# A hybrid DeltaNet / gating / SwiGLU layer: the input projection wholly in two-part products

## The chip, the cores and the metric

One core of a Trainium2 chip runs the whole program in one launch. The time is that of the device in microseconds (us), the median of several executions. Engines are named as in the profile: PE (TensorE: matmul), PEld (its weight load), DVE (VectorE), ACT (ScalarE), POOL (GpSimd) and SP (SyncE), which here issues every DMA, in order.

## What is computed

One layer over 2304 tokens (256 of context, 2048 latent), width 1024. The part that the change touches is the first third: the modulation vectors, the modulated RMSNorm and the input projection.

```python
mod = (jax.nn.silu(c) @ w_ada + b_ada)[:, None, :]
sh1, sc1, g1, sh2, sc2, g2 = jnp.split(mod, N_MOD, axis=-1)
h = rmsnorm(x, norm1_g) * (1 + sc1) + sh1
proj = h @ w_in        # 1024 x 3088: q, k, v, z (512 each), u, vb (512 each), 16 gate logits
...                    # conv + gated DeltaNet scans, spatial gating
y = jnp.concatenate([y_a, y_b.astype(h.dtype)], axis=-1) @ w_out
x = x + g1 * y
h = rmsnorm(x, norm2_g) * (1 + sc2) + sh2
x = x + g2 * swiglu(h, w_gate, w_up, w_down)
```

## The kernel before, in words

**Tiles and passes.** Tokens are cut into 6 groups of 384 (three tiles of 128). `PASSES` walks through them in 8 passes of 24, 24, 24, 12, 12, 24, 12 and 12 *blocks*, 144 in all. A block (`block_mm`) is 128 output columns of `w_in` for one group: 8 steps of 128 over the contraction, summed in one PSUM bank `pd` of 384 to 388 columns. Six passes begin with the 16 gate logits (`plg`, function `logits`). In the first two passes 14 and 18 *modulation pieces* stand between the blocks: a piece is 128 rows of `w_ada` by 1024 columns, multiplied by the two conditioning vectors.

**Two kinds of product.** In steps 0 to 3 of a block the weights `wraw` and activations `hT0` are plain float32; the profile shows two matmul records for each such product. In steps 4 to 7 both are cut into two parts of type float32r (a high part by a cast, a low part by subtraction), and a product is three matmuls: high x high, low x high, high x low. The parts of the weights lie in `whl`, those of the activations in the two tiles `hT1`. In the trace all of these read `pd<-hT,wraw` (float32) and `pd<-hT,whl` (parts). The pieces of the first pass go in parts (`ada<-whl,wlg`), those of the second as float32 (`ada<-wraw,wl`).

**How weights come.** An item of the stream is a block or a piece. On its first use (36 blocks) 512 KB of `w_in` come into one of four `wraw` buffers, four items ahead (`s_load`), and `s_split` makes the parts of rows 512 to 1023: a cast on ACT or DVE, a subtraction on DVE or POOL, into one of four `whl` buffers. The parts are also written to DRAM (`wp`, 512 KB); k, q and v in pass 0, vb, u and z in pass 1. The other 108 blocks (*kept* below) read 256 KB of float32 rows and 512 KB of finished parts.

**Order.** All engines' instructions stand in an order that a planner makes while the program is built: `Model` holds a clock for each engine, steps of the side work (`spawn`) become due by it, and `tick` puts them between the matmuls of the blocks. That side work is the convolutions, the preparation of the DeltaNet chunks (`pk`, `px`), and the scans. `h_put` turns the next group's activations into matmul form: the first half while the last block of a pass is at step 4, the second half behind that block. After the passes come the output projection (from about 1250 us) and the FFN, from 1591 us to the end.

Of the kernel before, what the change touches and what calls it, by code (L numbers as in the profile page):

```python
# [9 lines left out]
F32 = mybir.dt.float32  # L10
# [6 lines left out]
KB = 8  # L17
# [10 lines left out]
NACC, NTH, NRB = 5, 4, 3  # L28
# [132 lines left out]
def hybrid_step(  # L161
# [367 lines left out]
    wlg = cA.tile([P, KB, P], F32R, name="wlg")  # L529

    wl32 = cA.tile([P, 4, P], F32, name="wl32")
    hal32 = cA.tile([P, 4, 20], F32, name="hal32")
    hal = [cA.tile([P, 4, 20], F32R, name=f"hal{i}") for i in range(2)]
    hT0 = cA.tile([P, 4, GT * P + 4], F32, name="hT0")
    hT1 = [cA.tile([P, 4, GT * P + 4], F32R, name=f"hT1{i}") for i in range(2)]

    with tc.manual_schedule():
# [95 lines left out]
        def ada_finish2(vec, mrow):  # L633
            if vec in (2, 5):
                vi = 0 if vec == 2 else 1
                for i in range(2):
                    pg = pt_("pg")
                    nc.tensor.matmul(pg[0:2], sel, mrow[:, i * 512:(i + 1) * 512], start=True, stop=True)
                    gs = A.tile([2, 512], F32, tag="tok", name="gs", bufs=3)
                    nc.scalar.copy(gs, pg[0:2])  # L640
                    nc.sync.dma_start(gv_d[vi, :, i * 512:(i + 1) * 512], gs)
# [48 lines left out]
        def h_put(g, hs, q):  # L690
            o = bo(g)
            ks = slice(4 * q, 4 * q + 4)
            for l in range(GT):
                c = slice(o + l * P, o + (l + 1) * P)
                if q:
                    nc.scalar.copy(hT1[0][:, :, c], hs[l][:, ks])
                    lighter(512, GP_BIAS_H).tensor_sub(hT1[1][:, :, c], hs[l][:, ks], hT1[0][:, :, c])
                else:
                    copy(hT0[:, :, c], hs[l][:, ks])
            for x, h in ((hT1[0], hal[0]), (hT1[1], hal[1])) if q else ((hT0, hal32),):  # L700
                if g:
                    nc.vector.tensor_copy(x[:, :, 0:2], h[:, :, (2 if g == 1 else 4 * (g - 1)):][:, :, 0:2])
                if 0 < g < NG - 1:
                    nc.vector.tensor_copy(x[:, :, o + GT * P:o + GT * P + 2], h[:, :, 4 * g + 2:4 * g + 4])
# [21 lines left out]
        DEPTH = 4  # L726
# [4 lines left out]
        wp_d = {first[kd] + P * i: dram.tile([P, 2, 512], F32, name=f"wp{kd}{i}") for kd in first for i in range(4)}  # L731

        halves = [(i, n) for i, it in enumerate(stream) for n in range(2)
                  if (not it[0] if it[1] == "ada" else n and it[0] <= kept_in(it))]
        place = {h: j for j, h in enumerate(halves)}

        def s_load(i):
            if i < len(stream):
                g, kind, a, c0 = stream[i]
                t = A.tile([P, KB, P], F32, tag="wraw", name="wraw", bufs=DEPTH)  # L740
                if kind != "ada" and g > kept_in(stream[i]):
                    assert not missing[wp_d[c0].name]
                    nc.sync.dma_start(t[:, 0:4], w_in[0:512, c0:c0 + P].rearrange("(k p) c -> p k c", p=P))
                    hl = A.tile([P, 2, 4, P], F32R, tag="whl", name="whl", bufs=4)
                    nc.sync.dma_start(hl[:].rearrange("p i k c -> p i (k c)").bitcast(F32), wp_d[c0])
                    raws[i], splits[i, 1] = t, (hl[:, 0], hl[:, 1])
                    return
# [7 lines left out]
        def s_split(j):  # L755

            if j < len(halves):
                i, n = halves[j]
                while i not in raws:
                    yield 200  # L760
                raw = raws[i]
                yield [raw]
                hl = A.tile([P, 2, 4, P], F32R, tag="whl", name="whl", bufs=4)
                hi, lo = hl[:, 0], hl[:, 1]
                copy(hi, raw[:, 4 * n:4 * n + 4])
                yield
                lighter(512, GP_BIAS if stream[i][0] else GP_BIAS_FIRST).tensor_sub(lo, raw[:, 4 * n:4 * n + 4], hi)
                splits[i, n] = (hi, lo)
                if stream[i][1] != "ada":
                    if stream[i][0] == kept_in(stream[i]):  # L770
                        store(wp_d[stream[i][3]], hl[:].rearrange("p i k c -> p i (k c)").bitcast(F32))
                elif n:
                    del raws[i]
                    yield
                    s_load(i + DEPTH)

        for i in range(DEPTH):
            s_load(i)
# [28 lines left out]
        def constants():  # L807
# [9 lines left out]
            nc.vector.tensor_copy(wlg, zr[:, None, :].to_broadcast([P, KB, P]))  # L817
            nc.vector.tensor_copy(wl32, zr[:, None, :].to_broadcast([P, 4, P]))
            nc.vector.tensor_copy(wl32[:, :, 0:2], cs[:, :, 0:4].rearrange("p c k -> p k c"))
            nc.vector.tensor_copy(wl32[:, :, 64:66], cs[:, :, 4:].rearrange("p c k -> p k c"))  # L820
            nc.vector.tensor_copy(wlg[:, :, 0:2], cs.rearrange("p c k -> p k c"))
            nc.vector.tensor_sub(wlg[:, :, 2:4], cs.rearrange("p c k -> p k c"), wlg[:, :, 0:2])
            yield [lraw]
            nc.vector.tensor_copy(wl32[:, :, 32:48], lraw[:, 0:4])
            nc.vector.tensor_copy(wlg[:, 4:, 32:48], lraw[:, 4:])
            nc.vector.tensor_sub(wlg[:, 4:, 48:64], lraw[:, 4:], wlg[:, 4:, 32:48])
# [15 lines left out]
        for j in range(3):  # L842
            spawn(s_split(j))
# [11 lines left out]
        def modulate(k):  # L855
            for c0, c1 in ((0, NP), (NP, NH + 20)):
                c = cx(c0 // P)
                n = min(c1, NH + 2)
                if k < 4:
                    act = k % 2 == 0  # L860
                    if act:
                        nc.scalar.activation(hT0[:, k, c0:n], xr[:, k, c0:n], AF.Identity,
                                             scale=mod[:, 0, c, k:k + 1], bias=mod[:, 1, c, k:k + 1])
                    else:
                        nc.vector.tensor_scalar(hT0[:, k, c0:n], xr[:, k, c0:n], mod[:, 0, c, k:k + 1],
                                                mod[:, 1, c, k:k + 1], op0=ALU.mult, op1=ALU.add)
                    continue
                nc.scalar.activation(hT1[0][:, k - 4, c0:n], xr[:, k, c0:n], AF.Identity,
# [5 lines left out]
        for k in range(KB):  # L874
            if k + 1 < KB:
                modulate(k + 1)
            if k >= 4:
                nc.vector.tensor_sub(hT1[1][:, k - 4, 0:NH + 2], xr[:, k, 0:NH + 2], hT1[0][:, k - 4, 0:NH + 2])
        for k in range(4):
            nc.scalar.activation(hal32[:, k], xr[:, k, NH:NH + 20], AF.Identity,  # L880
                                 scale=mod[:, 0, 0, k:k + 1], bias=mod[:, 1, 0, k:k + 1])
        nc.scalar.copy(hal[0], xr[:, 4:, NH:NH + 20])
        nc.gpsimd.tensor_sub(hal[1], xr[:, 4:, NH:NH + 20], hal[0])
# [1496 lines left out]
```

## Time and profile before

| | us |
|---|---|
| median of 3 runs (3088.43 to 3098.06) | 3096.82 |
| the profiled execution | 3100.84 |
| its span, first to last instruction | 3098.8 |
| of which the 144 blocks, from 48.2 to 1222.3 | 1174.1 |

Share of the span: PE 95% busy, PEld 82%, DVE 67%, ACT 43%, POOL 12%. A busy time counts an engine as busy from an instruction's start to its modelled end, so a PE that waits inside a run of overlapping matmuls may still count as busy. The DMA share is the busy time of the core's 16 DMA engines by that of 16 that never pause; in a full stretch it reads slightly over 1. PEclk is the granted TensorE clock, 1.00 being 2.4 GHz and 0.50 being 1.2 GHz.

### The profile page before, as it was taken

Reading aid. Unit: us, or ns where it says so; the run is one execution under the profiler, and the core shown is the slowest. Engines: PE = TensorE matmul, PEld = TensorE weight load, DVE = VectorE, ACT = ScalarE, POOL = GpSimd, SP = SyncE. Lnnn points to the kernel's source line nnn. Section 1 sums busy time; section 2 is a strip of 40 time slices with the busy share of each in tenths; the row PEclk is TensorE's granted clock in tenths of the full one; section 3 lists DMA queues with packets and bytes.
Section 4 is the critical chain, followed back from the end, with each engine's and each line's share of the span. In section 5 each row is a group of like instructions: output and inputs, shape, how many; then the busy total and the mean of one; then the engine's idle time right before and its main releaser. Section 6 shows DMA issues by size and latency. Waiting matters only on the chain. (4 is left out here: it accounts for less than half of the span.)

```text
span 3098.8 us, 45733 instructions
## 1 busy us (share of the span) xinstructions
PE 2941.6 (95%) x15379; PEld 2543.6 (82%) x15379; DVE 2077.9 (67%) x3882; ACT 1331.0 (43%) x3056; POOL 375.6 (12%) x551
## 2 busy tenths in 40 slices
PE   8989999999889999899969999999999999999998
PEld 3666777877667788798759999999999998888887
DVE  3767457476548675565588888777768866467666
ACT  4754445545646433243253333344333333344443
POOL 1121211211212111122222211000000000000000
PEclk9989999999989999899979999999999999999999
DMA  7978998887789988896537777877789956567764
GB/s 251 349 240 241 285 305 250 297 245 229 228 271 265 286 257 259 293 347 228 175 125 226 223 207 241 271 224 219 200 268 329 319 164 216 171 200 245 224 217 174
DMA packets 764442, 756.23 MB, mean 244 GB/s; under 512 B 93194, under 2 KB 610831, under 8 KB 762929
## 3 DMA queue, kind: packets, MB, share of 16 engines
q1 hardware_dynamic: 764209, 753.31, 77.9%
q8 instruction: 123, 2.02, 0.3%
q14 instruction: 110, 0.90, 0.1%
HBM read 539.27 MB, written 213.90 MB: 243 GB/s over the span
## 5 line engine op out<-in xcount | busy, mean ns | idle before, releaser
L149 PE MATMUL pm<-hb,wu 128*128 128x384 f32 x5544 | 992.3, 340 | 22.1 <-DMA hb<-hbd 8.0
L149 PEld LDWEIGHTS pm<-hb,wu 128*128 128x128 f32 x5544 | 978.7, 189 | 28.6 <-issue 8.9
L149 PE MATMUL pm<-un,ah 128*128 128x512 f32 x2079 | 478.7, 392 | 4.6 <-DVE ah L149 2.1
L149 PEld LDWEIGHTS pm<-un,ah 128*128 128x128 f32 x2079 | 391.9, 189 | 91.2 <-DVE ah L149 2.5
L149 PE MATMUL pd<-hT,wraw 128*128 128x384 f32 (+2 forms) x1152 | 435.5, 502 | 18.4 <-ACT rb L149 10.6
L149 DVE TENSOR_TENSOR wu<-ws,wu 128x512 fp32r<-128x512 f32 x448 | 321.2, 717 | 125.5 <-ACT wu L149 121.0
L149 PE MATMUL pd<-hT,whl 128*128 128x384 f32 (+2 forms) x1728 | 396.3, 371 | 6.7 <-DVE whl L149 6.7
L149 PEld LDWEIGHTS pd<-hT,whl 128*128 128x128 f32 x1728 | 311.6, 195 | 37.2 <-DVE whl L149 8.3
L149 PEld LDWEIGHTS pd<-hT,wraw 128*128 128x128 f32 x1152 | 208.5, 195 | 116.7 <-ACT rb L149 12.6
L149 ACT CAST wu<-ws 128x512 fp32r<-128x512 f32 x448 | 255.2, 616 | 20.5 <-DVE ws L149 20.5
L149 DVE TENSOR_TENSOR u<-u,pm 128x384 f32<-128x384 f32 x264 | 144.5, 547 | 19.9 <-PE pm L149 19.9
L149 ACT ACTIVATE s<-s 128x384 f32<-128x384 f32 x66 | 34.7, 525 | 258.1 <-DVE s L149 258.1
L149 DVE SCALAR_TENSOR_TENSOR acc<-rb,colT,acc 128x384 f32<-128x384 f32 (+1 forms) x252 | 138.9, 580 | 9.1 <-POOL acc L149 8.8
L149 DVE TENSOR_TENSOR ah<-ar,ah 128x1408 fp32r<-128x1408 f32 x63 | 102.3, 1623 | 55.9 <-ACT ah L149 54.7
L149 ACT ACTIVATE u<-u 128x384 f32<-128x384 f32 x66 | 34.7, 525 | 231.2 <-DVE u L149 231.2
L149 ACT CAST ah<-ar 128x1408 fp32r<-128x1408 f32 x63 | 86.4, 1372 | 108.3 <-PE pm L149 93.3
L149 DVE TENSOR_TENSOR un<-ur,un 128x512 fp32r<-128x512 f32 x154 | 99.5, 685 | 23.2 <-ACT un L149 23.2
L149 POOL TENSOR_TENSOR acc<-acc,th 128x384 f32<-128x384 f32 (+2 forms) x43 | 50.5, 1175 | 447.0 <-ACT th L149 436.1
L149 PE MATMUL po<-woa,yhi 128*128 128x512 f32 x288 | 101.8, 404 | 1.8 <-DVE tm L149 1.8
L149 PE MATMUL po<-wob,yhi 128*128 128x512 f32 x288 | 102.4, 408 | 0.0
L149 ACT CAST un<-ur 128x512 fp32r<-128x512 f32 x154 | 87.8, 615 | 19.4 <-DMA ur<-in_w_down_dram 8.7
L149 DVE TENSOR_TENSOR C<-C,pm 128x512 f32<-128x512 f32 x63 | 42.4, 685 | 79.1 <-PE pm L149 78.8
(303 smaller groups left out, 4148.4 us busy)
## 6 DMA issues: line engine op xcount, KB each, us to landing
ws<-ws SPq DMA_DIRECT2D x256, 256.0 KB
ar<-fa SPq DMA_DIRECT2D x63, 704.0 KB
ws<-in_w_gate_dram SPq DMA_DIRECT2D x128, 256.0 KB
wraw<-in_w_in_dram SPq DMA_DIRECT2D x108, 256.0 KB
ur<-wt SPq DMA_DIRECT2D x88, 256.0 KB
ws<-in_w_up_dram SPq DMA_DIRECT2D x84, 256.0 KB
fa<-u SPq DMA_DIRECT2D x99, 192.0 KB
x<-in_x_sample_dram SPq DMA_DIRECT2D x37, 512.0 KB
```

Source lines behind the costliest of these rows:

```text
L149: fn(*a, **k)
```

## The change

All 8 steps of a block use two-part products: 24 matmuls in place of 4 float32 products and 12 matmuls. `hT0` and the two `hT1` become four float32r tiles `hT[q][i]`, `hal32` goes, `modulate` and `h_put` make a high and a low part for both halves. Both halves of a weight block are split on its first use and both are stored (two stores of 512 KB); a kept block reads two times 512 KB of parts and no float32 rows. All modulation pieces multiply float32 (`wc32`, 4 columns of weights in place of 64), so those of the first pass are no longer split. The logits use parts only, with 32 columns in place of 128. `wraw` has two buffers in place of four, `whl` six (`NHL`) in place of four; a kept half is loaded as soon as six halves ago is used up (`s_next`), and a raw item when one of the two buffers comes free: a block's when both its halves are split, a piece's when PE has multiplied it.

```diff
-    wlg = cA.tile([P, KB, P], F32R, name="wlg")
...
-    hT0 = cA.tile([P, 4, GT * P + 4], F32, name="hT0")
-    hT1 = [cA.tile([P, 4, GT * P + 4], F32R, name=f"hT1{i}") for i in range(2)]
+    wlg = cA.tile([P, KB, 36], F32R, name="wlg")
+    wc32 = cA.tile([P, KB, 4], F32, name="wc32")
+    hal = [cA.tile([P, KB, 20], F32R, name=f"hal{i}") for i in range(2)]
+    hT = [[cA.tile([P, 4, GT * P + 4], F32R, name=f"hT{q}{i}") for i in range(2)] for q in range(2)]
...
-                if q:
-                    nc.scalar.copy(hT1[0][:, :, c], hs[l][:, ks])
-                    lighter(512, GP_BIAS_H).tensor_sub(hT1[1][:, :, c], hs[l][:, ks], hT1[0][:, :, c])
-                else:
-                    copy(hT0[:, :, c], hs[l][:, ks])
+                nc.scalar.copy(hT[q][0][:, :, c], hs[l][:, ks])
+                lighter(512, GP_BIAS_H).tensor_sub(hT[q][1][:, :, c], hs[l][:, ks], hT[q][0][:, :, c])
...
-        DEPTH = 4
-        wp_d = {first[kd] + P * i: dram.tile([P, 2, 512], F32, name=f"wp{kd}{i}") for kd in first for i in range(4)}
+        kept = lambda it: it[1] != "ada" and it[0] > kept_in(it)
+        plain = lambda it: it[1] == "ada"
+        wp_d = {first[kd] + P * i: dram.tile([P, 2, 1024], F32, name=f"wp{kd}{i}") for kd in first for i in range(4)}
...
+        def s_next(free=True):
+
+            taken[2] -= free
+            while taken[1] < len(halves) and taken[2] < NHL:
+                i, n = halves[taken[1]]
+                taken[1] += 1
+                taken[2] += 1
+                hl = A.tile([P, 2, 4, P], F32R, tag="whl", name="whl", bufs=NHL)
+                if kept(stream[i]):
+                    src = wp_d[stream[i][3]]
+                    assert not missing[src.name]
+                    nc.sync.dma_start(hl[:].rearrange("p i k c -> p i (k c)").bitcast(F32), src[:, n])
+                    splits[i, n] = (hl[:, 0], hl[:, 1])
+                else:
+                    spawn(s_split(i, n, hl))
+
+        for i in range(2):
+            s_load()
...
-                if k < 4:
-                    while i not in raws:
-                        idle()
-                    until(raws[i], hT0)
-                    nc.tensor.matmul(ps[:, :n], raws[i][:, k], hT0[:, k, c0:c0 + n], start=(k == 0), stop=False)
...
+                q, kk = divmod(k, 4)
+                while (i, q) not in splits:
+                    idle()
+                hi, lo = splits[i, q]
+                until(hi, lo, *hT[q])
+                for j, (w, x) in enumerate(((hi, hT[q][0]), (lo, hT[q][0]), (hi, hT[q][1]))):
+                    nc.tensor.matmul(ps[:, :n], w[:, kk], x[:, kk, c0:c0 + n], start=(k == 0 and j == 0),
+                                     stop=(k == KB - 1 and j == 2))
+                if kk == 3:
+                    del splits[i, q]
+                    s_next()
...
-                        if pi:
+                        if True:
...
-                            nc.tensor.matmul(ada_ps[n][0:64], wl32[:, k % 4, k // 4 * 64:k // 4 * 64 + 64],
+                            nc.tensor.matmul(ada_ps[n][0:4], wc32[:, k],
                                              raws[i][:, 4 * n:4 * n + 4].rearrange("p k c -> p (k c)"),
```

On PE in pass 0, around the first modulation piece that stands between two blocks, before (`hT_262` is the float32 tile, `hT_263` and `hT_264` are the high and the low part):

```order
L149 MATMUL pd<-hT_264,whl 128x386
L149 MATMUL ada_753<-whl,wlg 64x512 x2
L149 MATMUL ada_754<-whl,wlg 64x512 x2
L149 MATMUL pd<-hT_262,wraw 128x386 x4
L149 MATMUL pd<-hT_263,whl 128x386 x2
L149 MATMUL pd<-hT_264,whl 128x386
```

and now (`hT_261` and `hT_262` are the parts of the first half, `hT_263` and `hT_264` those of the second):

```order
L149 MATMUL pd<-hT_264,whl 128x386
L149 MATMUL ada_784<-wraw,wc_258 4x512
L149 MATMUL ada_785<-wraw,wc_258 4x512
L149 MATMUL pd<-hT_261,whl 128x386 x2
L149 MATMUL pd<-hT_262,whl 128x386
```

The piece is two float32 products in place of four on parts, and the block behind it begins with parts.

On SP at the start of the stream, before:

```order
L149 DMA lraw<-in_w_in_dram 128x8x16
L149 DMA wraw<-in_w_in_dram 128x8x128 x2
L149 DMA wraw<-in_w_ada_dram 128x1024
L149 DMA wraw<-in_w_in_dram 128x8x128
L149 DMA wpk_361<-whl 128x1024
L149 DMA wpk_362<-whl 128x1024
```

and now:

```order
L149 DMA lraw<-in_w_in_dram 128x8x16
L149 DMA wraw<-in_w_in_dram 128x8x128 x2
L149 DMA wpk_361<-whl 128x1024 x2
L149 DMA wpk_362<-whl 128x1024 x2
L149 DMA wraw<-in_w_ada_dram 128x1024
L149 DMA wraw<-in_w_in_dram 128x8x128
```

The third and the fourth item stood ahead of the first stores, and now stand behind four of them.

On SP in pass 1, where kept blocks and pieces alternate, before:

```order
L149 DMA wraw<-in_w_in_dram 128x4x128
L149 DMA whl<-wpq_367 128x1024
L149 DMA wraw<-in_w_ada_dram 128x1024
L149 DMA wraw<-in_w_in_dram 128x4x128
L149 DMA whl<-wpq_368 128x1024
```

and now:

```order
L149 DMA whl<-wpq_365 128x1024 x2
L149 DMA wraw<-in_w_ada_dram 128x1024
L149 DMA whl<-wpq_366 128x1024 x2
L149 DMA wraw<-in_w_ada_dram 128x1024
L149 DMA mrow<-in_b_ada_dram 1x1024
```

The 256 KB of float32 rows have gone, and the parts are read two times 512 KB a block.

## Rows read from the trace of the kernel before

**Rows 1.** The page, part 1: busy time, share of the span, instructions.

```profile
PE 2941.6 (95%) x15379; PEld 2543.6 (82%) x15379; DVE 2077.9 (67%) x3882; ACT 1331.0 (43%) x3056; POOL 375.6 (12%) x551
```

**Rows 2.** Windows by pass: stretch, length, busy of each engine, PEclk, DMA share, GB/s.

```profile
48.20:238.10 189.90, 168.60 (x708) 124.28 (x707) 127.46 (x296) 122.37 (x320) 34.20 (x62) 0.92 0.85 277
238.10:446.50 208.40, 204.92 (x952) 144.45 (x952) 115.25 (x235) 98.33 (x238) 40.51 (x77) 0.98 0.93 282
446.50:634.80 188.30, 178.88 (x997) 147.96 (x996) 115.30 (x248) 90.47 (x253) 35.77 (x66) 0.98 0.86 266
634.80:719.50 84.70, 81.58 (x431) 64.81 (x429) 70.78 (x154) 44.87 (x123) 9.93 (x7) 1.00 0.81 231
719.50:829.70 110.20, 95.99 (x478) 77.58 (x479) 56.99 (x137) 60.29 (x182) 19.59 (x48) 0.92 0.78 245
829.70:1009.90 180.20, 162.12 (x808) 129.16 (x806) 116.30 (x251) 101.49 (x262) 36.52 (x51) 0.95 0.86 259
1009.90:1104.10 94.20, 89.72 (x494) 74.74 (x495) 65.81 (x120) 42.71 (x91) 15.62 (x37) 0.96 0.90 270
1104.10:1222.30 118.20, 117.78 (x788) 104.27 (x788) 70.24 (x142) 32.92 (x73) 22.85 (x71) 1.00 0.84 262
```

**Rows 3.** What PE waited for from 48 to 1222 us: total, times, longest (us).

```profile
PE px L149 <- DMA wbd<-w: 14.9, 6, 6.8
...
PE pd L149 <- DVE whl L149: 6.7, 3, 5.7
```

**Rows 4.** The same for SP's DMA queue.

```profile
SPq L149 <- PE pd L149: 242.2, 125, 8.9
```

**Rows 5.** PE in order of time, pass 1: start, length, what, count.

```profile
277.05 1.31 PE L149 MATMUL pd<-hT,whl 128*128 128x386 f32 x6
278.19 2.75 PE L149 MATMUL pd<-hT,wraw 128*128 128x386 f32 x8
280.49 2.56 PE L149 MATMUL pd<-hT,whl 128*128 128x386 f32 x12
282.98 1.93 PE L149 MATMUL ada<-wraw,wl 128*64 128x512 f32 x4
284.85 0.55 PE L149 MATMUL ptr<-ident,acc 128*128 128x128 f32 x3
```

**Rows 6.** PE in order of time, pass 0: a modulation piece in parts.

```profile
83.21 1.09 PE L149 MATMUL ada<-whl,wlg 128*64 128x512 f32 x4
84.14 2.76 PE L149 MATMUL pd<-hT,wraw 128*128 128x386 f32 x8
```

**Rows 7.** The chain of waits, in the FFN: start, length, what.

```profile
2290.99 298.83 PE pm L149 x1692
```

**Rows 8.** DMA issues of the run: what, count, KB each.

```profile
wraw<-in_w_in_dram SPq DMA_DIRECT2D x108, 256.0 KB
...
whl<-wpk SPq DMA_DIRECT2D x20, 512.0 KB
...
wpk<-whl SPq DMA_DIRECT2D x4, 512.0 KB
```

**Rows 9.** Windows with the DMA engines full, columns as in rows 2.

```profile
100.00:150.00 50.00, 48.77 (x223) 36.25 (x222) 33.05 (x81) 38.46 (x114) 5.23 (x13) 1.00 1.05 352
1300.00:1400.00 100.00, 99.04 (x701) 91.30 (x701) 59.59 (x155) 41.71 (x168) 26.72 (x21) 1.00 1.03 344
```

**Rows 10.** Tile `whl`, 48 to 1222 us: ns min/median/max; last, idle before splits.

```profile
L149 DVE TENSOR_TENSOR whl<-wraw,whl x52: 675/684/1115, 55.2 to 432.7; 128x512 fp32r<-128x512 f32 x52
L149 ACT CAST whl<-wraw x33: 602/615/636, 54.5 to 407.8; 128x512 fp32r<-128x512 f32 x33
...
  DMA wraw<-in_w_in_dram: 7.5, 5
```

**Rows 11.** ACT in order of time where pass 0 begins.

```profile
46.39 5.38 ACT L149 ACTIVATE hT<-xr,mod 128x256 f32<-128x256 f32 x12 [1.65 <-DVE mod L149]
```

**Rows 12.** PE in order of time where pass 6 begins.

```profile
1009.92 2.20 PE L149 MATMUL pd<-hT,wraw 128*128 128x384 f32 x6 [1.26 <-ACT hT L149]
```

More of the change, by code (lines that the diff above doesn't have):

```diff
@@ L725, in hybrid_step, with s_load @@
         raws, splits = {}, {}
-        DEPTH = 4
         second = next(pi for pi in range(1, len(PASSES)) if PASSES[pi][1] != "delta")
         kept_in = lambda it: second if it[1] in ("vb", "u", "z") else 0
-        wp_d = {first[kd] + P * i: dram.tile([P, 2, 512], F32, name=f"wp{kd}{i}") for kd in first for i in range(4)}
[L733 to L738, printed above, removed]
-                g, kind, a, c0 = stream[i]
[L740 to L747, printed above, removed]
+        kept = lambda it: it[1] != "ada" and it[0] > kept_in(it)
+        plain = lambda it: it[1] == "ada"
+        wp_d = {first[kd] + P * i: dram.tile([P, 2, 1024], F32, name=f"wp{kd}{i}") for kd in first for i in range(4)}
+        whole = [i for i, it in enumerate(stream) if not kept(it)]
+        halves = [(i, n) for i, it in enumerate(stream) if not plain(it) for n in range(2)]
+        taken = [0, 0, 0]
+        def s_load():
+            if taken[0] < len(whole):
+                i = whole[taken[0]]
+                taken[0] += 1
+                g, kind, a, c0 = stream[i]
+                t = A.tile([P, KB, P], F32, tag="wraw", name="wraw", bufs=2)
                 if kind == "ada":
@@ L753, in s_load @@
                 raws[i] = t
-        def s_split(j):
-            if j < len(halves):
-                i, n = halves[j]
-                while i not in raws:
[L760 to L765, printed above, removed]
-                yield
[L767 to L775, printed above, removed]
@@ L777, in hybrid_step, with s_split @@
-        for i in range(DEPTH):
-            s_load(i)
+        def s_split(i, n, hl):
+            while i not in raws:
+                yield 200
+            raw = raws[i]
+            yield [raw]
+            hi, lo = hl[:, 0], hl[:, 1]
+            copy(hi, raw[:, 4 * n:4 * n + 4])
+            yield
+            lighter(512, GP_BIAS if stream[i][0] else GP_BIAS_FIRST).tensor_sub(lo, raw[:, 4 * n:4 * n + 4], hi)
+            splits[i, n] = (hi, lo)
+            if stream[i][1] != "ada" and stream[i][0] == kept_in(stream[i]):
+                store(wp_d[stream[i][3]][:, n], hl[:].rearrange("p i k c -> p (i k c)").bitcast(F32))
+            if n:
+                del raws[i]
+                yield
+                s_load()
@@ L841, in hybrid_step @@
         spawn(constants(), set_up)
-        for j in range(3):
-            spawn(s_split(j))
+        s_next(False)
         for vec in (1, 0):
@@ L876, in hybrid_step @@
                 modulate(k + 1)
[L877 to L883, printed above, removed]
+            nc.vector.tensor_sub(hT[k // 4][1][:, k % 4, 0:NH + 2], xr[:, k, 0:NH + 2], hT[k // 4][0][:, k % 4, 0:NH + 2])
+        nc.scalar.copy(hal[0], xr[:, :, NH:NH + 20])
+        nc.gpsimd.tensor_sub(hal[1], xr[:, :, NH:NH + 20], hal[0])
         phP.close()
@@ L1481, in logits @@
                     def logits(k):
[L1482 to L1489 removed]
+                        q, kk = divmod(k, 4)
+                        until(*hT[q])
+                        for i in range(2):
+                            nc.tensor.matmul(pl[0:32, :nrow], wlg[:, k, 0:32], hT[q][i][:, kk, o:o + nrow],
+                                             start=(k + i == 0), stop=(k + i == KB))
                         if k % 2:
```

81 lines of the change are left out of this document (23 added, 58 removed).

## The prediction

> **What bounds the kernel now.** I read the page first: PE is busy 95% of the span [rows 1], and no other engine comes near. The change lies in the blocks of passes 0 to 7, so the windows by pass come next [rows 2]. The reader is to see two things in them. PE is the busiest engine in every pass, at 87 to 100% of its length; DVE has a sixth to a half of its time free and ACT a third or more. And the DMA share, 0.78 to 0.93, leaves little: where the engines are full, the share reads 1.03 to 1.05 at 344 to 352 GB/s [rows 9], so 335 GB/s is one full share. Length times share gives the DMA time of passes 0 to 7: 161, 194, 162, 69, 86, 155, 85 and 99 us, 1011 in all. PE's own waits are short: 15 us for `wbd`, which the preparation reads back, 7 us for `whl` [rows 3]. SP in turn waited 242 us for PE to free a buffer [rows 4]: loads are issued as soon as there is room, and their landing is hidden by how far ahead they go. So PE sets the pace, with the DMA engines close behind.
>
> **The change part by part: PE.** In a clean block the float32 half starts at 278.19, the half in parts at 280.49, the next thing at 282.98: 4.79 us for 386 columns [rows 5]. The new block is 24 products in parts. One end of their price is the FFN's undisturbed run, 298.83 us by 1692, 0.177 us each [rows 7], 4.24 us a block. The other is a short run of this projection, six products behind a transpose, 278.19 - 277.05 = 1.14 us, 0.19 each [rows 5], 4.56 us. The saving is 0.23 to 0.55 us a block; I take 0.48 (0.18 a product), since 24 products in a row are nearer to the long run. 144 blocks: -69 us, with bounds of -33 and -79. The logits of a pass trade 4 float32 products (2.3 us to the next start, 2.75 to their own end [rows 5], so some 2.5) for 8 in parts (1.4), -1.1 each, six times, -7. A modulation piece in parts takes 84.14 - 83.21 = 0.93 us [rows 6], as float32 284.85 - 282.98 = 1.87 [rows 5]: 14 pieces, +13. Sum on PE: -63; by pass 0, -13, -13, -7, -7, -13, -6, -6 (the logits counted where they stand, the 13 us of the pieces in pass 0).
>
> **DMA.** The 108 kept blocks drop a read of 256 KB and add one of 512 KB (`whl` is read 108 times now, in six groups like the one shown) [rows 8]: +256 KB each, 0.78 us at 335 GB/s. The 24 stores of parts double (six groups of four): +512 KB, 1.57 us each. Lower prices are possible, since the dropped rows were short pieces; higher ones too, since pass 1 moves only 282/0.93 = 303 GB/s per share. Added time by pass: 12 stores 19; 12 kept and 12 stores 28; 24 kept 19; 12 kept 9; 9; 19; 9; 9: 122 us. The DMA time becomes 180, 222, 181, 78, 95, 174, 94, 108.
>
> **The sum.** PE alone would need 190, 196, 176, 78, 103, 168, 88 and 112 us. At a share of 1.05 the transfers need 171, 211, 172, 74, 90, 166, 90, 103; the later of the two in each pass adds up to 1128, against 1174 now: -46. At a share of 1.00 the sum is 1154, -20. A whole pass has never run at 1.05, and one reached 0.93, so both ends are hopeful; I take the middle, -33.
>
> **DVE, ACT and SP.** Pass 0 splits 24 more halves of blocks and 28 fewer of pieces, pass 1 12 more; at 0.62 for the cast and 0.68 for the subtraction [rows 10] that is 16 us of work in 208, on two engines half free: nothing, unless a split comes late (below). At each of the 7 changes of group three subtractions are added (0.68 each), and the four float32 steps (2.5 us) that cover the second half's casts become 2.1 us. The change to pass 6 already shows 1.26 us of waiting for `hT` [rows 12]. I put 0.7 us on each, +5; the bounds are 0 and 2.5 (all of it bare). At the start ACT makes 16 in place of 12 activations, 7.2 in place of 5.4 us [rows 11], and DVE 8 more operations, but the first block also gets shorter: nothing, within 2 us. SP loses one issue and gains one in a kept block. In passes 0 and 1 raw buffers fall from four to two, and a store can stand ahead of the next load: +6 here, bounds 0 and 50 (third rival).
>
> Sum: -33 + 5 + 6 = -22 us. From the profiled execution, 3100.84 (its span of 3098.8 and 2 us around it), that is 3079; the median of the runs shown is 4.0 below it, so 3075. The output projection and the FFN are left as they are.
>
> **Rivals.** *First, PE's whole saving arrives.* For it: in the window from 100 to 150 us the share is 1.05 and PE still works 48.77 of 50 us at full clock, and so from 1300 to 1400 [rows 9]; three blocks of parts stand ready, some 20 us of PE. It needs the added transfers to go into the quarter of the DMA time that is idle now. Price: -63 + 3 = -60, 3037. The Trainium skill, "DMA: Bandwidth & Descriptors", section Specifications, limits a core to about 358 GB/s of its memory, which the 352 in rows 9 agrees with. By that figure pass 1 would need (58.8 + 9.4) MB / 358 = 190 us, less than PE's 196, and the time would be this rival's.
>
> *Second, the DMA engines take it all.* The passes' shares stop at about 0.96, since SP issues in order and waits in front of buffers: 1133/0.96 = 1180 us against 1174, with the +5 and some of PE's cover, 3097 to 3108. That the change doesn't do what it says ends here too: in passes full of side work, products in parts at 0.19 us each save only 0.23 a block, -33 + 6, and the DMA costs eat the rest.
>
> *Third, the shorter look-ahead costs more than all that, slower.* Place: passes 0 and 1, behind modulation pieces. A piece keeps one of the two `wraw` buffers until PE has multiplied it; the next block's load is then issued, has to land, be cast (0.62) and subtracted (0.68), within the block and the piece that are left to PE, 4.3 + 1.9 = 6.2 us. Four buffers deep, splits already stood idle for `wraw` 7.5 us in five waits [rows 10], and PE 6.7 us for `whl` [rows 3]. A load of 512 KB takes 1.6 us at full share, behind whatever is queued. If load and split together take 6.2 us nothing is lost; at 7.3 us, 1.1 us on each of some 23 such places (14 pieces in pass 0, 9 in pass 1) makes 25 us and brings the time back to before, and from there on the kernel is slower. At 8.3 us it is 48 us, 3117. Against it: side work on PE lengthens a block to 7.9 us in pass 0 and 8.7 in pass 1 [rows 2].
>
> **How the numbers follow.** The forecast, part of the saving (3055 to 3088), has a chance of 0.37; the first rival (3030 to 3055) 0.17; the second (3088 to 3106) 0.19; the third (3106 to 3150) 0.27. A measurement of this kernel tells about 0.3%, 9.3 us, from no change, so below 3087.5 is faster, above 3106.1 slower: 0.53, 0.20, 0.27. The likeliest gives 3075. For 8 in 10 the range leaves out the lower third of the first rival and about half of the third: 3036 to 3124.
>
> **What would show it.** Blocks of 4.3 us with no float32 products; DMA shares of 0.95 to 1.02 in passes 1, 2, 5 and 6, with pass 1 no shorter than now and passes 2 to 7 some 5 us shorter each. The first rival shows in shares of 1.02 and more in all passes and a pass 1 of 196 us; the second in PE's waits for DMAs (`wbd`, `skq`) growing from 15 us to 50; the third in waits of `pd` for `whl` in passes 0 and 1, with both longer than before, and a lower PEclk there. I am wrong in the main if pass 1 falls clearly, or if passes 2 to 7 grow.

## The result, and the profile after

The changed kernel takes 3145.25 us (median of 4 runs, 3143.51 to 3146.22), the kernel before 3097.44 beside it: a ratio of 1.0158, with an interval from 1.0135 to 1.0181. It is slower by 48 us, where 22 us less were forecast. (Such intervals, at 95%, stand in square brackets below.) Its page, part 1 (busy time, share of the span, instructions), answers to [rows 1]:

```profile
PE 2910.0 (93%) x15955; PEld 2638.3 (84%) x15955; DVE 2103.9 (67%) x3915; ACT 1339.4 (43%) x3049; POOL 397.2 (13%) x566
```

PE is busy 32 us less, in a span 44 us longer. Where the time went shows in the windows by pass of the changed kernel, which answer to [rows 2] (stretch, length, busy of PE, PEld, DVE, ACT, POOL, PEclk, DMA share, GB/s); the last row is the stage from the last block to the FFN:

```profile
48.30:275.20 226.90, 179.03 (x803) 137.76 (x801) 138.94 (x311) 128.65 (x321) 42.46 (x72) 0.90 0.87 282
275.20:498.20 223.00, 199.80 (x1038) 158.23 (x1038) 123.98 (x248) 99.33 (x242) 43.22 (x80) 0.95 0.90 287
498.20:685.90 187.70, 175.44 (x1163) 170.52 (x1163) 106.21 (x246) 93.52 (x260) 32.08 (x64) 0.97 0.94 313
685.90:783.30 97.40, 76.98 (x439) 73.40 (x439) 74.15 (x154) 48.54 (x134) 18.32 (x21) 0.89 0.78 235
783.30:885.70 102.40, 92.18 (x586) 87.75 (x585) 64.22 (x157) 59.65 (x164) 23.53 (x44) 0.93 0.92 309
885.70:1059.40 173.70, 151.44 (x872) 145.60 (x870) 120.27 (x240) 98.68 (x254) 35.08 (x44) 0.92 0.96 300
1059.40:1147.40 88.00, 82.44 (x516) 79.77 (x515) 61.11 (x114) 39.15 (x83) 19.75 (x39) 0.96 0.94 292
1147.40:1262.90 115.50, 105.56 (x742) 104.39 (x743) 67.74 (x133) 30.77 (x66) 20.69 (x66) 0.96 0.83 261
1262.90:1639.70 376.80, 335.83 (x1958) 291.49 (x1956) 224.09 (x448) 131.66 (x420) 94.63 (x80) 0.94 0.75 250
```

Against [rows 2], pass 0 is 37 us longer, pass 1 15, pass 3 13. Passes 2 and 4 to 7 are 1, 8, 7, 6 and 3 us shorter. The stage behind the passes (368.5 us before) is 8 us longer, the FFN 5 shorter. The blocks themselves did become shorter; a run of PE without a break, in order of time (start, length, what):

```profile
1021.74 6.09 PE L149 MATMUL pd<-hT,whl 128*128 128x384 f32 x33
```

That is 0.185 us a product with the last one counted to its own end (a product by itself takes a median of 0.338 us), or 0.180 from one start to the next: 4.32 to 4.43 us for a block's 24 of 384 columns, where the clean block before, of 386, took 4.79 [rows 5]. PE's waits grew. In pass 0 PE now waits for the splits (total, times, longest, us), 6.7 us before [rows 3]:

```profile
PE pd L149 <- DVE whl L149: 25.6, 16, 4.9
```

And the tile `wraw` in pass 0 of the changed kernel tells why these are late (loads with their count; what the engines that use it sat idle for, us and times; then the time from issue to landing, least, median and longest):

```profile
L149 SPq DMA_DIRECT2D wraw<-in_w_in_dram x21: 368/384/1145, 58.0 to 255.5; - x21
L149 SPq DMA_DIRECT2D wraw<-in_w_ada_dram x15: 327/333/986, 67.4 to 269.1; - x15
...
  DMA wraw<-in_w_in_dram: 45.2, 21
...
DMA to landing us min/median/max: 4.0/5.4/8.7
```

36 loads in 226.9 us through two buffers: each buffer takes a new load every 12.6 us on average, and of these the load itself takes 5.4 by the median.

### The profile page after: what moved, and what is told of

Same layout as the page of the kernel before. It is cut to its first block, busy times and chain, and to the rows that moved or that the text cites. A ratio compares the mean times of both kernels' runs of the same rounds, so it can differ in the third digit from the quotient of the medians.

```text
span 3143.1 us, 46924 instructions
## 1 busy us (share of the span) xinstructions
PE 2910.0 (93%) x15955; PEld 2638.3 (84%) x15955; DVE 2103.9 (67%) x3915; ACT 1339.4 (43%) x3049; POOL 397.2 (13%) x566
## 5 line engine op out<-in xcount | busy, mean ns | idle before, releaser
L149 PE MATMUL pd<-hT,whl 128*128 128x384 f32 (+2 forms) x3456 | 729.3, 360 | 67.5 <-DVE whl L149 27.8
L149 PEld LDWEIGHTS pd<-hT,whl 128*128 128x128 f32 x3456 | 629.5, 198 | 98.0 <-DVE whl L149 27.6
L149 POOL TENSOR_TENSOR ws<-ws 128x512 f32<-128x512 f32 x40 | 63.2, 1580 | 263.3 <-DMA ws<-in_w_up_dram 155.4
L149 PE MATMUL ph<-ident,x 128*128 128x128 f32 x336 | 55.9, 294 | 32.8 <-DVE x L149 14.6
```

The costliest lines, as they stand in the source:

```text
L149: fn(*a, **k)
```

## Experiments on the buffers

Six kernels change only what lies between the loads and PE. Theory: passes 0 and 1 are longer since two raw buffers look less far ahead than four. Rivals: the splits are late by themselves, or the stores of parts fill the DMA engines.

**e1**, the changed kernel with four raw and four half buffers:

```diff
-NACC, NTH, NRB, NHL = 5, 4, 3, 6
+NACC, NTH, NRB, NHL = 5, 4, 3, 4
...
-                t = A.tile([P, KB, P], F32, tag="wraw", name="wraw", bufs=2)
+                t = A.tile([P, KB, P], F32, tag="wraw", name="wraw", bufs=4)
```

> The changed kernel with four raw buffers again and four halves of parts in place of two and six (the same memory). If the short look-ahead for raw weights behind modulation pieces made passes 0 and 1 longer (+37 and +15 us in the profiles), they return to some 190 and 200 us and the time is 3085 to 3105. If it is the added DMA traffic or the splits on DVE and ACT, passes 0 and 1 stay at 220 to 227 and 215 to 223 us, and the time stays within 10 us of 3145, or rises since kept blocks have only four halves ahead.

Measured: 3151.6 us, ratio 1.0195 [1.0178, 1.0212]. Its windows (columns as above; passes 0 and 1, pass 5, the stage behind the passes):

```profile
49.10:234.30 185.20, 164.55 (x804) 127.02 (x803) 120.63 (x278) 117.56 (x307) 43.97 (x68) 0.96 0.95 319
234.30:454.50 220.20, 196.74 (x997) 155.97 (x996) 122.07 (x243) 102.22 (x250) 47.05 (x83) 0.92 0.91 289
...
842.60:1052.50 209.90, 168.16 (x974) 161.24 (x972) 129.47 (x274) 102.90 (x260) 35.19 (x61) 0.90 0.89 271
1250.80:1638.00 387.20, 342.21 (x2022) 299.08 (x2021) 228.92 (x459) 133.96 (x425) 97.51 (x90) 0.93 0.75 248
```

Pass 0 comes back, 185.2 us, shorter than before. Pass 1, which was to come back too, stays at 220.2: more raw buffers do not mend it. And 36 us more in pass 5 and 10 behind the passes take it away again: the FFN starts at 1638.0, in the changed kernel at 1639.7. **e2** (the pieces of pass 0 in parts again), **e3** (two buffers for pieces, two for blocks) and **e4** (one of the two stores, the other half's parts used twice) are variants of the same question:

```diff
-        plain = lambda it: it[1] == "ada"
+        plain = lambda it: it[1] == "ada" and it[0]
...
-                t = A.tile([P, KB, P], F32, tag="wraw", name="wraw", bufs=2)
+                t = A.tile([P, KB, P], F32, tag=("wraw", "araw")[c], name="wraw", bufs=2)
...
-            if stream[i][1] != "ada" and stream[i][0] == kept_in(stream[i]):
+            if n and stream[i][1] != "ada" and stream[i][0] == kept_in(stream[i]):
```

> The changed kernel with the pieces of pass 0 in parts again, as before the change (buffers two and six). Look-ahead theory: a piece of pass 0 no longer keeps a raw buffer until PE comes to it, so pass 0 falls by 20 to 35 us, pass 1 does not change: 3110 to 3125. If the float32 pieces cost only their own time on PE, pass 0 falls by 13 us at most: 3132 or more. If the splits on DVE and ACT are what is late, pass 0 grows (28 more halves): above 3145.

> The changed kernel with two buffers for the pieces and two for raw blocks, each loaded in its own order, and four halves of parts: no piece can keep a block's buffer. Look-ahead theory: passes 0 and 1 as with four raw buffers or better, 3085 to 3100. If it is DMA traffic or splits: 3135 to 3155.

> The changed kernel, but only the second half of the parts is stored (24 stores of 512 KB as before the change), and kept blocks read that half twice; so their first four steps use the wrong weights. DMA theory: 19 us less transfer in each of passes 0 and 1, and the time falls by 20 to 38 us, to 3107 to 3125. Look-ahead theory: the stores are not what is waited for, the time falls by 0 to 8 us.

Measured: 3160.21, 3178.02 and 3163.31 us, 15, 33 and 18 more than the changed kernel; e3 and e4 lie above everything that was expected of them. With the pieces of pass 0 in parts (e2) that pass falls by 7 us only, to 220.1, and the rest of the kernel loses more. Pass 0 falls to 196.4 us with buffers of their own for the pieces (e3), and again nothing is left of it at the end. 12.6 MB of stores less gain nothing (e4): that rival falls.

**e5** joins both sizes of the look-ahead: four raw and four half buffers until the last raw item, then all eight for halves.

```diff
+                tag = "wraw" if taken[1] > last and (taken[1] - last) % 2 else "whl"
+                if flight[tag] + (len(raws) if tag == "wraw" else 0) >= 4:
+                    break
...
-                hl = A.tile([P, 2, 4, P], F32R, tag="whl", name="whl", bufs=NHL)
+                hl = A.tile([P, 2, 4, P], F32R, tag=tag, name="whl", bufs=4)
```

> Four buffers for raw items and four for halves as long as items come raw (passes 0 and 1), and from the last raw item on all eight hold halves (a half then goes by turns into a former raw buffer). Nothing is left out. Look-ahead theory: both sizes of the look-ahead count, each in its own passes. With four raw buffers pass 0 took 185.2 us in place of 226.9, and with four half buffers pass 5 took 209.9 in place of 173.7; with the two joined pass 0 is 183 to 192, pass 1 stays near 220, and passes 2 to 7 are no longer than in the changed kernel: 3085 to 3110 us in all. Order theory (the planner's order of side work is simply worse with two more splits per block, and a gain in one pass is lost in another): 3135 to 3160 as in the runs so far.

Measured: 3163.11 us [1.0194, 1.0247]. Pass 0 is 189.8 us, as expected; pass 5 is 194.5 and the stage behind the passes 395.6. The total is just above the band of the order theory. The look-ahead theory's second half falls: more half buffers do not bring pass 5 back to 173.7. **e7** tests the first half by itself: the kernel before with two raw buffers (`DEPTH = 2`).

> The kernel before with two buffers for raw items in place of four, nothing else. Look-ahead theory: pass 0 alone, where no block is kept, grows from 190 us to 225 to 240, since an item is fetched, waited for and split before the buffer comes free; later passes grow too, as the float32 rows of kept blocks use the same buffers, and the total is 3150 to 3300. Order theory: two buffers do not matter by themselves, pass 0 stays at 190 to 200.

Measured: 3182.84 us [1.0264, 1.0305]. Its pass 0:

```profile
48.00:273.50 225.50, 177.51 (x707) 122.95 (x706) 143.13 (x310) 133.38 (x333) 51.47 (x75) 0.91 0.79 247
```

225.5 us against 189.9 [rows 2], with the old products: 36 us, and e1 takes 42 off again, so the two buffers by themselves account for pass 0's 37. They are not the loss of the kernel, since e1, e3 and e5 repaired pass 0 and ended no earlier.

## Experiments on PE's work

If pass 0 can lose and win 40 us without the end moving, PE's blocks may not set the end at all. **e11** takes the PE's saving of the change alone:

```diff
-                    for j, (w, x) in enumerate(((hi, hT1[0]), (lo, hT1[0]), (hi, hT1[1]))):
+                    for j, (w, x) in enumerate(() if kk == 3 else ((hi, hT1[0]), (lo, hT1[0]), (hi, hT1[1]))):
...
```

> The kernel before with the last step of the contraction left out of every block (three matmuls on parts of 13 + 8 loads per block, 0.177 us each, 76 us in all 144), the transfers and splits as before: the PE's saving of the change (69 us) without anything else of it. If the blocks' PE time sets the end: 65 to 80 us less than before, 3015 to 3030. If it is set by the side work between the blocks (the steps of DVE, ACT and the transfers, for which the PE waits sooner when its blocks are shorter): 0 to 35 us less, 3060 to 3095, and the PE's waits grow by what its work shrinks.

Measured: 3106.35 us, ratio 1.0037 [1.0023, 1.0052]. 76 us less work on PE, and the kernel is 11 us slower, outside both bands. **e14** puts the same 76 us on top:

```diff
+                    if kk == 2:
+                        for w, x in ((hi, hT1[0]), (lo, hT1[0]), (hi, hT1[1])):
+                            nc.tensor.matmul(ps[:, :n], w[:, kk], x[:, kk, c0:c0 + n], start=False, stop=False)
```

> The kernel before with the three matmuls on parts of step 6 done twice in every block: 15 in place of 12 (the product of that step counts twice in the sum), 76 us of PE work more, nothing else. If the PE sets the pace in most passes: 55 to 76 us more, 3150 to 3172. If the side work sets it in the same measure as it hid the saving: 0 to 30 us more, 3096 to 3126.

Measured: 3161.43 us [1.0181, 1.0237], 66 us more. So the kernel before stands at a knee: more PE work costs nearly all of itself, less gives nothing. Windows of the passes and the stage behind them: the row of the passes (columns as above) and the sum of both stretches (length, busy of the engines); first the kernel before, then e11, then e14 (sum alone), then the changed kernel:

```profile
48.20:1222.30 1174.10, 1099.58 (x5645) 867.24 (x5644) 738.14 (x1580) 593.45 (x1539) 214.99 (x418) 0.96 0.86 265
...
sum 1542.60, PE 1425.75 PEld 1149.46 DVE 954.99 ACT 723.04 POOL 308.40; mean PE 712.87 PEld 574.73 DVE 477.49 ACT 361.52 POOL 154.20
```

```profile
48.90:1210.10 1161.20, 1028.65 (x5043) 782.41 (x5041) 740.18 (x1560) 578.97 (x1498) 216.87 (x407) 0.94 0.85 262
...
sum 1548.00, PE 1376.84 PEld 1085.16 DVE 966.95 ACT 713.53 POOL 317.59; mean PE 688.42 PEld 542.58 DVE 483.48 ACT 356.77 POOL 158.80
```

```profile
sum 1600.30, PE 1488.90 PEld 1217.55 DVE 960.53 ACT 726.79 POOL 305.03; mean PE 744.45 PEld 608.78 DVE 480.26 ACT 363.39 POOL 152.51
```

```profile
48.30:1262.90 1214.60, 1062.87 (x6149) 957.43 (x6148) 756.63 (x1599) 598.29 (x1522) 235.13 (x428) 0.94 0.90 287
...
sum 1591.40, PE 1398.70 PEld 1248.92 DVE 980.71 ACT 729.96 POOL 329.76; mean PE 699.35 PEld 624.46 DVE 490.36 ACT 364.98 POOL 164.88
```

The difference of the first two numbers is PE idle: 117 us before, 171 in e11, 111 in e14, 193 in the changed kernel. So of e11's 76 us PE gives 54 back as waiting. The rest goes in slower work: its busy time shrinks by 49 us only, with the granted clock of the passes at 0.94 in place of 0.96. Span times what the mean clock (0.973 before, 0.964 in e11, 0.963 in the changed kernel) lacks of 1.00 puts that at some 28 us in e11 and 33 in the changed kernel, an estimate from above, since part of it falls into idle time. PE's lines in the stage behind the passes show where the rest went (count, then busy us and mean ns); first the kernel before, then e11:

```profile
L149 PE MATMUL px<-xx,z 128*128 128x32 f32 (+1 forms) x56 | 7.5, 280 | 1.5 <-DVE xx L149 1.5
```

```profile
L149 PE MATMUL px<-xx,z 128*128 128x64 f32 (+1 forms) x96 | 11.6, 270 | 0.0
```

`px` belongs to the preparation of the DeltaNet chunks, side work that stands between the blocks. Less of it stands between the shorter blocks of e11, and what does not stand there stands behind the passes: e11's passes are 13 us shorter (1161.2 against 1174.1), and its stage behind them is 18 us longer (386.8 against 368.5). In the changed kernel 64 of these products are left, in e14 none. This order is fixed when the program is built: it is the planner, by its modelled clock, that leaves the steps over. No run here shows whether the engines could have done them earlier in another order.

## Experiments on the parts of the change

Base for the next three is **e8**, the kernel before with one part of the change alone, the float32 pieces in pass 0:

```diff
-                  if (not it[0] if it[1] == "ada" else n and it[0] <= kept_in(it))]
+                  if it[1] != "ada" and n and it[0] <= kept_in(it)]
...
-                        if pi:
+                        if True:
```

> The kernel before, with the modulation pieces of pass 0 as float32 (as in pass 1 there), nothing else: 28 casts and 28 subtractions fewer, and two float32 products in place of four on parts for each of the 14 pieces. By the prediction's term for the pieces (+13 us on PE) pass 0 is 190 to 203 us and the total 3092 to 3106. Rival: the splits that go away were late, so pass 0 loses some of its 7 us of waits for whl and the total is 3080 to 3090.

Measured: 3076.64 us, ratio 0.9945 [0.9925, 0.9966]: 18 us faster, what its rival expected and a little more. PE spends more on each piece, but 28 halves need no splitting, and pass 0 is 180.6 us. **e16** adds the other splits of the change, without use for their result:

```diff
+                copy(hi, raw[:, 0:4])
+                yield
+                lighter(512, GP_BIAS if stream[i][0] else GP_BIAS_FIRST).tensor_sub(lo, raw[:, 0:4], hi)
                 copy(hi, raw[:, 4 * n:4 * n + 4])
```

> The kernel before with float32 pieces in pass 0 (3077 us), and in each of the 36 first uses the first half of the raw block is cast and subtracted too, into the same buffer, before the second half's split overwrites it: 36 casts and 36 subtractions more, some 0.6 and 0.7 us each, 47 us over three engines, none of which is needed by anyone. If the splits make the side work late: 25 to 50 us more, in passes 0 and 1 and in what is left for the stage behind the passes. If they fit into the gaps of DVE and ACT: within 15 us of 3077.

Measured: 3124.76 us, 48 more than e8. Its passes 0 and 1, 20 and 21.5 us longer than in e8 (180.6 and 202.0):

```profile
53.40:253.80 200.40, 182.07 (x707) 120.66 (x706) 118.83 (x284) 122.68 (x314) 31.71 (x64) 0.94 0.85 271
253.80:477.30 223.50, 206.63 (x944) 143.98 (x943) 119.51 (x239) 96.44 (x238) 43.73 (x81) 0.97 0.80 251
```

DVE is busy 59% of pass 0 and ACT 61%. Its 24 casts and 24 subtractions more are 31 us at [rows 10], which fit several times into the idle time of the two, and still the pass is 20 us longer. PE's waits for `whl` grow from 0.9 us in the passes of e8 to 11.8, and its clock in pass 0 falls from 0.99 to 0.94. That the added steps stand in the order ahead of steps that others wait for would explain it; no run takes that apart. Pass 1's loss in the changed kernel, which four raw buffers did not take back, has its match here. **e17** adds the bytes:

```diff
-                    nc.sync.dma_start(t[:, 0:4], w_in[0:512, c0:c0 + P].rearrange("(k p) c -> p k c", p=P))
+                    nc.sync.dma_start(t, w_in[:, c0:c0 + P].rearrange("(k p) c -> p k c", p=P))
```

> The same base (3077 us), and each of the 108 kept blocks reads its whole 512 KB of float32 rows in place of 256 KB: 1 MB per kept block as in the changed kernel, 28 MB more, some 100 us of the DMA engines, the added rows used by nobody. If the bytes count: 20 to 60 us more. If they are hidden: within 12 us of 3077.

Measured: 3113.10 us, 36 more. The added rows come in pieces of 128 columns, so this is not the form that the bytes have in the changed kernel. The passes are as long as in e8 (1153.6 us against 1156.0); the stage behind them has 39 us more:

```profile
1203.90:1599.00 395.10, 348.63 (x2070) 303.25 (x2069) 226.70 (x468) 134.61 (x427) 103.03 (x107) 0.95 0.76 256
```

Here too the loss stands behind the passes, with 104 products `px<-xx,z` in place of e8's 55. **e18** takes all of it at once: e16's splits, e17's bytes, e11's shorter blocks and, at each change of group, a second operation on the first half of the activations:

```diff
-                    copy(hT0[:, :, c], hs[l][:, ks])
+                    lighter(512, GP_BIAS_H).tensor_sub(hT0[:, :, c], hs[l][:, ks], hs[l][:, 4:8])
+                    nc.scalar.copy(hT0[:, :, c], hs[l][:, ks])
```

> The same base with all of it at once: the splits of the first halves, the bytes, an additional subtraction for the first half of the activations at each group change, and the last step of the contraction left out of every block (76 us of PE work less). Four raw buffers stay. If these account for the loss of the change: 3130 to 3165, as the whole contraction in parts had with four raw buffers (3152 and 3163). If the loss is in the buffers or in the order alone: 3065 to 3100.

Measured: 3136.50 us, ratio 1.0127 [1.0105, 1.0148]. With four raw buffers and float32 products, 39 us of the change's loss of 48 are there. The single parts give -18 + 48 + 36 + 0 = 66, all together 39: they overlap, or the orders differ (below). The added operation at the change of group was not tried by itself.

## Experiments on SP's queue and the bytes

SP issues in order, and a kept read at its head waits until PE frees the buffer. **e6** cuts bytes (half of each kept read, on e5); **e9** and **e10** put the kept reads on the queue 4 us later by the planner's clock, on e5 and e8; **e13** and **e12** do e6's and e11's cut on top of these; **e15** is e10 with 8 us.

```diff
-                    nc.sync.dma_start(hl[:].rearrange("p i k c -> p (i k c)").bitcast(F32), src[:, n])
-                    splits[i, n] = (hl[:, 0], hl[:, 1])
+                    nc.sync.dma_start(hl[:, 0].rearrange("p k c -> p (k c)").bitcast(F32), src[:, n, 0:512])
+                    splits[i, n] = (hl[:, 0], hl[:, 0])
...
-                        s_load(i + DEPTH)
+                        if i + DEPTH < len(stream) and stream[i + DEPTH][1] != "ada" and stream[i + DEPTH][0] > kept_in(stream[i + DEPTH]):
+                            at(model.clock + DEFER, lambda j=i + DEPTH: s_load(j))
+                        else:
+                            s_load(i + DEPTH)
```

> The kernel with the switched buffers, but a kept half reads only its high part (256 KB in place of 512 KB) and multiplies it in place of the low part too, so the low part of the kept weights is left out of the sum; the PE does the same number of matmuls. DMA theory: passes 1 to 7 are held by the DMA engines (pass 1 took 220 to 226 us in every version so far at a share of 0.84 to 0.91); 57 MB less, at the 290 GB/s of these passes some 190 us of transfers, lets pass 1 fall to about 200 and passes 2 to 7 by another 20 to 40 us, total 40 to 60 below the switched kernel. Theory of latencies and side work (the passes end by waits of single steps for ACT, DVE and the reads of the scans, not by bytes): within 15 us of the switched kernel, and pass 1 stays above 212.

> The kernel with the switched buffers (3163 us), and the read of a kept half is put on SP's queue 4 us later by the planner's clock than the matmul that frees its buffer; nothing else. Queue theory: in the switched kernel SP waits 293 us in all for the PE to free a buffer, and behind it stand the stores and reads of the side work (at 916 us in the run with half the kept bytes, ACT had sat idle 7.8 us for a store of the convolution, behind a read of parts that waited for the PE). With the wait mostly over when the read comes to the head, SP's wait for pd falls below 150 us and the total by 20 to 60 us. Rival (the side work is late for reasons of its own, and the queue only shows it): SP's wait falls, the total stays within 12 us of 3163.

> The kernel before with float32 pieces in pass 0 (3077 us), and the reads for a kept block are put on SP's queue 4 us later; four items lie ahead, so PE should not come to wait for them. Queue theory: SP's wait for pd (237 us there) falls below 120 us and the total by 10 to 40 us, to 3037 to 3067. Rival: within 8 us of 3077.

> The kernel before with float32 pieces in pass 0 and later reads (3057 us), with the last step of the contraction left out of every block: 9 matmuls on parts in place of 12, 76 us of PE work less in 144 blocks. If SP's queue was what held the side work back when blocks became shorter: the saving comes through, 40 to 76 us less, 2981 to 3017. If the side work's own chain (DVE, ACT, latencies of the reads) sets the pace: within 20 us of 3057, with more waits of the PE for gx, rb, xx and zz.

> The whole contraction in parts with switched buffers and later reads (3132 us), a kept half reading only its high part, which is multiplied in place of the low part too (the low part of the kept weights is left out of the sum). If the bytes hold it: 57 MB less, 40 to 75 us less, 3057 to 3092. If the side work does: within 20 us of 3132. Without later reads the same cut gave 32 us.

> The kernel before with float32 pieces in pass 0 and the reads for kept blocks 8 us later in place of 4. Queue theory: SP's wait for the PE, 89 us with 4, falls below 50, and the total by 0 to 15 us, to 3042 to 3057. Rival: the weights come late now (four items are some 30 us), or it is within 6 us of 3057.

Measured:

| | us | against its base |
|---|---|---|
| e6, half the kept bytes | 3130.80 | -32 (e5) |
| e9, reads 4 us later | 3132.33 | -31 (e5) |
| e13, e9 and half the kept bytes | 3119.75 | -13 (e9) |
| e10, reads 4 us later | 3057.08 | -20 (e8) |
| e12, e10 and 76 us less on PE | 3055.14 | -2 (e10) |
| e15, reads 8 us later | 3080.83 | +24 (e10) |

SP's wait for PE, in e5, e9, e10 and e15 (total, times, longest, us):

```profile
SPq L149 <- PE pd L149: 292.9, 131, 14.0
```

```profile
SPq L151 <- PE pd L151: 103.3, 66, 5.3
```

```profile
SPq L151 <- PE pd L151: 88.6, 72, 6.0
```

```profile
SPq L151 <- PE pd L151: 78.2, 51, 8.9
```

Later reads paid in both bases, as the queue theory said, and e10 is the fastest kernel here: 0.9878 [0.9854, 0.9902] of the kernel before. But e15 misses: the same idea 4 us further loses 24 us, with hardly any waiting of PE for weights. A change of due times gives all engines another order, and it seems that orders alone can differ by that much; so the size of the queue's part stays open, and so do the smaller single differences above (e2, e4, e8, e13): only those well over 24 us say much. The place at 916 us that e9's expectation quotes was read wrongly: a store of `acc` had been issued at 911.08 us, ahead of the read that waited, and ACT went on at 916.24, so its 7.8 us are mostly landing time. Of the bytes, e6 gained 32 us, between what its two theories said, and e13 13, in the band of the side work. e13 moves 287 MB in its passes (1160.2 us at 247 GB/s), the kernel before 311 (1174.1 at 265), and it is still 24 us slower than that.

e12 repeats e11 where SP no longer waits long for PE (107 us), and again 76 us of PE work are worth nothing. Its rows of the passes and of passes and stage behind, after those of e10:

```profile
50.30:1195.40 1145.10, 1104.29 (x5781) 864.50 (x5780) 723.83 (x1566) 585.94 (x1504) 219.54 (x429) 0.99 0.88 274
...
sum 1495.50, PE 1411.59 PEld 1129.51 DVE 934.63 ACT 712.55 POOL 308.61; mean PE 705.80 PEld 564.76 DVE 467.32 ACT 356.27 POOL 154.31
```

```profile
51.70:1156.10 1104.40, 1022.51 (x5037) 770.18 (x5036) 707.38 (x1532) 568.93 (x1472) 191.31 (x385) 0.95 0.88 273
...
sum 1503.30, PE 1380.84 PEld 1082.58 DVE 930.23 ACT 703.34 POOL 297.44; mean PE 690.42 PEld 541.29 DVE 465.12 ACT 351.67 POOL 148.72
```

The passes of e12 are 41 us shorter than e10's (1104.4 against 1145.1), and the stage behind is 48 us longer (398.9 against 350.4); there stand 96 products `px<-xx,z` where e10 has none:

```profile
L151 PE MATMUL px<-xx,z 128*128 128x64 f32 (+1 forms) x96 | 12.9, 284 | 0.0
```

Here PE's idle time grows by 39 us and its busy time shrinks by 31 in place of 76, with the clock of the passes at 0.95 after 0.99 (by the mean clocks of the two runs, 0.982 and 0.969, some 40 us). What the passes of e12 wait for more is ACT, which empties a block's bank (`rb`, `gx`); in e10 the two are 8.5 and 3.0 us:

```profile
PE pd L151 <- ACT gx L151: 18.1, 5, 8.7
PE pd L151 <- ACT rb L151: 17.6, 6, 8.1
```

So less waiting of SP for PE does not let the saving through either. The reading that fits all of this is that the side work has a pace of its own, PE waits for it when its blocks are shorter, and the clock falls with the waiting. Which step sets that pace, on the engines or in the planner's order, no run here took apart.

## Why the prediction was wrong

**What bounds the kernel.** "PE sets the pace, with the DMA engines close behind" is the step that failed. It was read from PE's busy share and its short waits. The runs show a knee: PE work counts when it grows (e14, 66 us for 76) and not when it shrinks (e11 +11 us, e12 -2). What PE saved came back as idle time (54 and 39 us) and as slower work at a lower clock. The prediction asked of each pass only when PE and when the DMA engines would be done, and never when the side work would be. Its rows of PE's waits leave out the second longest, 10.6 us for ACT's `rb`, one of the two that grew in e12:

```profile
PE pd L149 <- ACT rb L149: 10.6, 4, 7.5
```

**PE's terms.** The sizes were near. A clean block takes 4.32 to 4.43 us, 0.36 to 0.47 less than before, where 0.48 was put: 52 to 68 us in 144 blocks. With the logits and the pieces the sum on PE was -63; PE's busy time in passes and stage behind fell by 27 (1425.8 to 1398.7), at the lower clock. The pieces' +13 on PE was not the kernel's: e8 gains 18 us, and the splits that they no longer need are the likely reason.

**DMA.** The time of the transfers grew from 1174.1 x 0.86 = 1010 us in the passes to 1214.6 x 0.90 = 1093 (the windows above, taken as one), by 83 where 122 was put. No pass came over a share of 0.96, and pass 1 has 0.90. The Trainium skill, "DMA: Bandwidth & Descriptors", section Specifications, gives a core about 358 GB/s; the prediction worked out from it, as an estimate, what pass 1 would need, 190 us. Pass 1 took 223 us at 287 GB/s, so that figure did not bind it. Nor is it a ceiling for a stretch here: e10 reached 366 GB/s in 50 us.

```profile
1250.00:1300.00 50.00, 49.66 (x325) 44.62 (x324) 30.43 (x74) 19.13 (x75) 13.73 (x10) 1.00 1.08 366
```

**The sum.** "The later of the two in each pass", -33, was the term that decided. No run measures it alone; the PE work in it, taken out without any other part of the change, gave +11 and -2 us. Passes 2 and 4 to 7 did lose 24 us, close to the forecast's 5 each, but pass 3 and the stage behind took 21 of them.

**DVE, ACT and SP.** "On two engines half free: nothing, unless a split comes late" is the second step that failed. The term set the added splits against those that went; by the runs the first cost 48 us (e16) and the change to float32 pieces gave 18 (e8), some 30 in place of nothing. For the change of group +5 was put; PE's waits for `hT` in the passes grew from 2.3 to 9.9 us, near it. The +6 for the raw look-ahead (bounds 0 and 50) measured 36 and 42 us in pass 0, by e7 and e1. Load and split, which were to decide between 6.2 and 8.3 us a place, are 6.7 us by the medians (5.4, 0.62 and 0.68) and 10 with the longest load; the round of 12.6 us holds other waits too, which the prediction did not count.

**The rivals.** The result lies in the third rival's band (3106 to 3150), and its signs are all there: waits of `pd` for `whl` in pass 0, longer passes 0 and 1, PEclk 0.90 and 0.95 in place of 0.92 and 0.98. Its mechanism is real and makes pass 0 what it is. But as the cause of the 48 us it doesn't hold, since e1, e3 and e5 take it away and stay at 3152 to 3178; that the time fell into its band is luck. The first rival, PE's whole saving, is the one that e11 refutes most plainly.

## What to carry to other kernels

Before a saving on the busiest engine is priced, take as much of its work out as the change would, and leave all else: here one such run would have turned the forecast. Where side work is woven between the blocks of a busy engine, count what of it is left when the blocks end; a shorter stage ahead of a longer one is no gain. Idle time of an engine is no proof that new steps are free: 31 us of them cost pass 0 20 us here, with several times as much idle time on their engines.

## What was not expected of the hardware

The share of time that the DMA engines reach with this mix stayed at 0.96 or less over every whole pass of the changed kernel, at up to 313 GB/s, though the stretches of 50 and 100 us in [rows 9] show up to 1.05 and 352. In the changed kernel the reads of kept parts took a median of 4.4 to 7.2 us from issue to landing, the same 512 KB each (page, part 6: count, KB, us):

```profile
whl<-wpk SPq DMA_DIRECT2D x40, 512.0 KB, 4.4
whl<-wpq SPq DMA_DIRECT2D x40, 512.0 KB, 6.2
whl<-wpv SPq DMA_DIRECT2D x40, 512.0 KB, 7.2
```

And the granted clock takes part in the exchange: with 76 us less work on PE it fell from 0.96 to 0.94 over the passes (e11) and from 0.99 to 0.95 (e12), and with 76 us more it read 0.98 (e14):

```profile
47.50:1288.70 1241.20, 1175.01 (x6229) 948.28 (x6228) 747.68 (x1596) 600.63 (x1534) 212.39 (x427) 0.98 0.83 255
```
